# Weight sums by accumulating transfers in a seven-product feed-forward kernel

## The chip, the cores and the metric

One core of a Trainium2 chip runs the whole kernel in one launch. The metric is the device time of one execution in microseconds, the median of the runs shown.

## The reference

Two layers of a streaming encoder. Each layer adds half a SwiGLU, then a token mixer (a Mamba-2 scan of 8 heads and an HGRN2 scan of 4 heads, side by side, from one input projection and into one output projection), then half a second SwiGLU. All is float32, over 592 tokens (16 meta, 512 prompt, 64 sample) and 1024 features, with 2816 hidden features in each SwiGLU.

```python
def _swiglu(x, w_gate, w_up, w_down):
    return (jax.nn.silu(x @ w_gate) * (x @ w_up)) @ w_down
...
for l in range(DEPTH):
    h = h + 0.5 * _swiglu(_rmsnorm(h, ln_ffa_w[l]), ffa_w_gate[l], ffa_w_up[l], ffa_w_down[l])
    m, c, s, g = _mixer(_rmsnorm(h, ln_mix_w[l]), ...)
    h = h + m
    h = h + 0.5 * _swiglu(_rmsnorm(h, ln_ffb_w[l]), ffb_w_gate[l], ffb_w_up[l], ffb_w_down[l])
```

## The kernel before

**Products.** Activations lie with features on partitions and tokens along the free dimension. A float32 operand is split into a high part (`wh`, `qh`, type fp32r) and a low rest (`wl`, `ql`); each product is three matmuls: high by high, high by low, low by high (lines 649 to 651 and 675 to 677).

**Quads.** In a SwiGLU, blocks of weights and halves of activations are combined as in Strassen's and Winograd's method: a 2 by 2 block product takes seven products in place of eight. Such a step is a `Quad` (line 434). The order of its seven products and their operands is the list `QUAD`; `product_quad` (line 661) issues them into PSUM tiles `pq` (gate and up) or `pd` (down). Of the seven weight operands three are raw blocks (`g1`, `g2`, `u2`), and four are sums: `s1 = u1 + u2`, `s2 = s1 + g1`, `s4 = s2 + g2`, `s3 = g1 + u1`. A gate/up step covers one block of 128 hidden features; its weight blocks are 128 by 512 (256 KB). A down step covers two blocks of 128 output features, with weight blocks of 128 by 384 or 128 by 256 by the number of hidden chunks. The first two hidden blocks of a feed-forward block are plain jobs (`pg`, `pu`, line 642). A feed-forward block alternates stretches: gate/up steps until a group of hidden blocks is ready, then four down steps over the group.

**The weights' way.** `fetch` (line 506) runs through all jobs and, for a quad, `fetch_quad` (line 563) loads `g1`, `u1`, `u2`, `g2` with four SP transfers into `raw` tiles (`wr`, six buffers). `combine` (line 579) forms the four sums on VectorE into `zq` tiles (`ws`, four buffers). `convert` (line 588) makes of each operand the high part on ACT (line 598) into one of six `hi` tiles and the low part on VectorE (line 602) into one of six `lo` tiles; these come free when the product is issued. So a step has four sums and seven low parts on VectorE, and besides the evacuations: in a gate/up step lines 897 to 919, in a down step seven additions to `h` (line 1013). Gates make a product wait until the earlier content of its PSUM tile has been read.

**The order of work.** Every task is a Python generator that yields (engine, estimated ns, events to wait for, buffers needed). `Plan.run` (line 170) simulates the engines with these estimates at build time and emits each piece in the order in which it could start; that fixes the order of every engine's queue, SP's and POOL's included. On the chip the queues run in that order, and an instruction that waits holds those behind it. A tile of a tag takes one of the tag's buffers and waits for the release of what lay there.

**Mixer.** The convolution of one of eight channel tiles (`conv`, line 1142) writes a projected tile `u` and an accumulator `cacc`, both in the large pool `T` (52 buffers of 128 by 592), and ends with a Silu. `near` (line 1396) copies a query tile into `qd`, of which there is one buffer; it and `v_t` and `k_t` (one buffer each) also hold some of the hidden tiles of a feed-forward block. `states` (line 1452) loads a sample state `hss` from memory, then forms the final states in `hfin`. `load_scalars` (line 280) loads and prepares the small parameters.

Of the kernel before, what the change touches and what calls it, by code (L numbers as in the profile page):

```python
# [16 lines left out]
P = 128  # L17
# [20 lines left out]
BLK = ((0, 128), (128, 128), (256, 128), (384, 128), (512, 80))  # L38
NT = 52
UK = 4  # L40
# [157 lines left out]
def body(ctx: ExitStack, tc: tile.TileContext, a: dict, o: dict):  # L198
# [19 lines left out]
    bet = Buf(sb, "etot", 2, [P, 6], F32)  # L218
    bhs = Buf(sb, "hss", 2, [P, P], F32)
    bb = Buf(sb, "b_t", 2, [P, 256], F32)  # L220
# [59 lines left out]
    def load_scalars():  # L280
# [22 lines left out]

        t = yield V, 1500, (t,), (bT,)
        tmp = bT.tile("lbt", [P, 10, 4])
# [3 lines left out]
        V.tensor_tensor(sc[:, 1], r0, sc[:, 0], op=ALU.subtract)  # L309
        V.tensor_tensor(sc[:, 2], r1, sc[:, 0], op=ALU.subtract)  # L310
        S.activation(sc[:, 1:3], sc[:, 1:3], AF.Exp)
        V.tensor_tensor(sc[:, 3], sc[:, 1], sc[:, 2], op=ALU.add)
        V.reciprocal(sc[:, 3], sc[:, 3])
# [8 lines left out]
        V.tensor_scalar(lg[:, 1], lb, 1e-30, 2.0 ** -60, op0=ALU.max, op1=ALU.min)  # L322
        V.tensor_scalar(lg[:, 1], lg[:, 1], 2.0 ** 60, None, op0=ALU.mult)
        S.activation(lg, lg, AF.Ln)
        V.tensor_tensor(lna, lg[:, 0], lg[:, 1], op=ALU.add)
        V.tensor_scalar(nlna, lna, -1.0, None, op0=ALU.mult)
        V.tensor_scalar(lnc, lb, -1.0, 1.0, op0=ALU.mult, op1=ALU.add)
        S.activation(lnc, lnc, AF.Ln)
        bT.put(t + 1000)
        lb_ev.set(t + 1000)  # L330

# [66 lines left out]
    def near(order):  # L398
        return 1e-3 * order
# [106 lines left out]
    def fetch():  # L506
# [9 lines left out]
        for i, job in enumerate(jobs):  # L516
            if isinstance(job, Quad):
                yield from fetch_quad(i, job, chain)
                continue
            src = job.src.rearrange("(k p) c -> p k c", p=P)  # L520
            for k0, k1, u in job.units:
                if job.whole:
                    if i == 0:
                        yield from whole(i, job, src, k0, k1, u, chain)
                    else:
                        plan.add(near(job.order), whole(i, job, src, k0, k1, u, chain))
                    if i == 0:
                        for b, g in ((0, 1), (1, 1), (2, 1)) if k0 == 0 else ():
                            yield from fetch_x(b, g)
                    continue  # L530
                t = yield "DMA", 190 * (k1 - k0), (), (braw,)
                raw = braw.tile(f"wr{i}", [P, k1 - k0, src.shape[2]])
                SP.dma_start(raw, src[:, k0:k1])
                t += 2000.0
                if job.few:
                    plan.add(near(job.order), convert_few(i, job, u, raw, t, chain))
                else:
                    plan.add(near(job.order), convert(u, raw, chain, braw.put, t))
            if i == 1:
                for b, g in ((3, 0), (4, 0), (3, 1), (4, 1)):  # L540
                    yield from fetch_x(b, g)
                t = yield "DMA", 380, ()
                SP.dma_start(cf[:, P:], a["c_f"][:, P:3 * P])
                cf_ev.set(t + 2000)
                load_params()
# [11 lines left out]
    def scaled(norm, k0, k1, u, t):  # L557
# [3 lines left out]
        u.ready.set(t)  # L561

    def fetch_quad(i, job, chain):
        nk = job.mix.nk
        got = {}
        for name, src in (("g1", job.wg[0]), ("u1", job.wu[0]), ("u2", job.wu[1]), ("g2", job.wg[1])):
            t = yield "DMA", 190 * nk, (), (braw,)
            raw = braw.tile(f"wr{i}", [P, nk, P])
            SP.dma_start(raw, src)
            got[name] = [raw, Ev(), Ev({"g1": 3}.get(name, 2), braw.put)]  # L570
            got[name][1].set(t + 2000.0)
        for name, n in (("s1", 2), ("s2", 2), ("s4", 1), ("s3", 1)):
            got[name] = [None, Ev(), Ev(n, bzq.put)]
        plan.add(near(job.order), combine(i, nk, got))
        for k, ((name, _, _), u) in enumerate(zip(QUAD, job.units)):
            raw, ev, use = got[name]
            plan.add(near(job.order + k), convert(u, got[name], chain, use.set, ev))

    def combine(i, nk, got):
        for name, p, q in (("s1", "u1", "u2"), ("s2", "s1", "g1"), ("s4", "s2", "g2"), ("s3", "g1", "u1")):  # L580
            t = yield V, ns_dve(nk * P), (got[p][1], got[q][1]), (bzq,)
            dst = got[name][0] = bzq.tile(f"ws{i}", [P, nk, P])
            V.tensor_tensor(dst, got[p][0], got[q][0], op=ALU.add)  # L583
            got[name][1].set(t)
            got[p][2].set(t)
            got[q][2].set(t)

    def convert(u, raw, chain, done, *waits):
# [510 lines left out]
    def mixer(l, norm, nxt, hv_out):  # L1099
# [42 lines left out]
        def conv(c):  # L1142
# [3 lines left out]
            def sink(hf, sl, pt, t):  # L1146

                r = norm.rstd
                if hf == 0:
                    t = yield V, ns_dve(HT), (t, norm.done, col_ev["cw"]), (bT,)  # L1150
                    u = ut["u"] = bT.tile("u", [P, 601])
                    V.tensor_tensor(u[:, 3:3 + HT], pt, r[:, 0:HT], op=ALU.mult)
                    bmm.put(t)
                    ut["made"].set(t)
                    G.memset(u[:, 0:3], 0.0)
                    G.tensor_copy(u[:, 515:518], col["st"][:, 24 * l + c:24 * l + 24:8])
                    return
# [10 lines left out]
                cb = col["cb"][:, 8 * l + c:8 * l + c + 1]  # L1168
                t = yield (V, S), (501, ns_act(598) + 90), (t,), (bT,)
                acc = bT.tile("cacc", [P, 598])  # L1170
                if plan.pick == 0:
# [3 lines left out]
                for k in range(1, 4):  # L1175
                    t = yield V, ns_dve(650), (t,)
                    V.scalar_tensor_tensor(acc, u[:, k:k + 598], cw[k], acc, op0=ALU.mult, op1=ALU.add)
                bT.put(t)
                t = yield S, 880, (t,), (bT,)
# [3 lines left out]
                S.activation(dst[:, 576:592], acc[:, 582:598], AF.Silu)  # L1183
                bT.put(t)
                v = (x4 if c < 4 else bc4)[c % 4]
# [210 lines left out]
        def near(e, c):  # L1396


            t = yield (S, G), (ns_act(512), ns_pool(512)), (qev[c],), (bqd,)
            qd = bqd.tile(f"qd{c}")  # L1400
# [51 lines left out]
        def states(e, c):  # L1452

            t = yield "DMA", 200, (e.cum_ev,), (bhs,)
            e.ssam = bhs.tile("hss")
            SP.dma_start(e.ssam, a["state_hgrn"][l, 0, c])
            d = t + 2000
            t = yield PE, ns_mm(P, 6), (e.kt_ev, e.vt_ev), (baux, baux, bT, bT)
            e.st = bT.tile("hst", [P, 4, P])
            fin = bT.tile("hfin", [P, 2, P])  # L1460
            pn, p4 = baux.tile("pn"), baux.tile("pn4")
# [19 lines left out]
            SP.dma_start(o["hgrn_p"][l, 0, c], fin[:, 1])  # L1481
            bT.put(t + 2500)

        def outputs(e, c):
# [12 lines left out]
            bT.put(t, 2)  # L1497
            bhs.put(t)

# [498 lines left out]
```

## Time and profile before

| | |
|---|---|
| runs | 2338.93 us median of 3 (2338.72 to 2342.32) |
| profiled execution | 2340.86 us, span 2339.1 us |
| mean granted TensorE clock | 0.992 |
| TensorE matmul busy | 2268.3 us, 97% |
| TensorE weight load busy | 2183.7 us, 93% |
| VectorE (DVE) busy | 2027.6 us, 87% |
| ScalarE (ACT) busy | 1211.7 us, 52% |
| GpSimd (POOL) busy | 123.0 us, 5% |
| transfers | 188.28 MB, 28.1% of 16 engines' span on SP's queue |

The span goes from the first to the last instruction; the execution's own time is 1.8 us longer. Busy times are those of recorded instructions; matmuls overlap one another, and so do consecutive instructions of VectorE, so that durations add up to more than the time between starts. The rows on which the prediction rests stand below, after the change.

### The profile page before, as it was taken

How to read it: one execution, taken by the hardware profiler on the slowest of the kernel's cores; microseconds unless marked ns; L12 is line 12 of the kernel's file. 1: busy time of each engine (PE TensorE's matmuls, PEld its weight loads, DVE VectorE, ACT ScalarE, POOL GpSimd, SP SyncE). 2: the span in 40 equal slices, each digit the busy share in tenths (PEclk: the TensorE clock that was granted, in tenths of full speed). 3: DMA queues.
4: the chain of work that ended last, by engine and by line, in shares of the span. 5: the costliest groups of instructions: out<-in, count | busy, mean ns of one | idle time of the engine just before them, and what ended most of it. 6: DMA issues, size and time to landing. Idle time of an engine off the chain costs nothing.

```text
span 2339.1 us, 43538 instructions
## 1 busy us (share of the span) xinstructions
PE 2268.3 (97%) x16199; PEld 2183.7 (93%) x16199; DVE 2027.6 (87%) x4224; ACT 1211.7 (52%) x2486; POOL 123.0 (5%) x167
## 2 busy tenths in 40 slices
PE   8989999999899999999999999999998999999998
PEld 6989999999899899999979999999997998999998
DVE  6989989768976899998989999896789678999995
ACT  4545645546443355564545556464563534555653
POOL 0000000021300000000000000000212000000002
PEclk9999999999999999999999999999999999999999
DMA  4233332332112123323222323323311231233332
GB/s 119 82 96 88 87 95 77 96 80 60 31 43 82 55 82 100 91 82 100 74 71 85 101 86 90 92 81 92 82 44 33 57 89 55 82 109 91 87 98 75
DMA packets 370243, 188.28 MB, mean 80 GB/s; under 512 B 16544, under 2 KB 367568, under 8 KB 370032
## 3 DMA queue, kind: packets, MB, share of 16 engines
q1 hardware_dynamic: 370032, 185.50, 28.1%
q8 instruction: 128, 2.10, 0.4%
q14 instruction: 83, 0.68, 0.1%
HBM read 180.94 MB, written 4.51 MB: 79 GB/s over the span
## 4 chain that ended last, share of the span: by engine, by line
PE 61%; DVE 28%; DMA 6%; issue 4%; ACT 1%; SPq 0%; POOL 0%; DVEq 0%; ACTq 0%
PE pq L675 8%; PE pq L677 8%; PE pq L676 8%; DVE wl L602 7%; DVE ws L583 5%; PE pd L675 4%; PE pd L676 3%; PE pd L677 3%; DVE h L1013 3%; DMA wr<-in_ffa_w_up 2%; DMA wr<-in_ffb_w_up 2%; PE pa L1380 2%; PE px L649 1%; PE px L651 1%; PE px L650 1%
## 5 line engine op out<-in xcount | busy, mean ns | idle before, releaser
L598 ACT ACTIVATE wh<-ws 128x512 fp32r<-128x512 f32 (+2 forms) x560 | 321.8, 575 | 272.8 <-PE pd L676 119.0
L598 ACT ACTIVATE wh<-wr 128x512 fp32r<-128x512 f32 (+2 forms) x572 | 333.2, 587 | 218.0 <-PE pd L676 87.8
L602 DVE TENSOR_TENSOR wl<-wr,wh 128x512 fp32r<-128x512 f32 (+2 forms) x572 | 358.9, 640 | 6.4 <-ACT wh L598 4.4
L602 DVE TENSOR_TENSOR wl<-ws,wh 128x512 fp32r<-128x512 f32 (+2 forms) x560 | 339.2, 616 | 18.6 <-ACT wh L598 17.4
L675 PE MATMUL pd<-qh_g,wh 128*128 128x296 f32 (+1 forms) x1008 | 306.6, 304 | 11.6 <-DVE h L1013 7.8
L676 PE MATMUL pd<-ql_g,wh 128*128 128x296 f32 (+1 forms) x1008 | 301.8, 299 | 4.1 <-DVE ql_g L500 4.1
L677 PE MATMUL pd<-qh_g,wl 128*128 128x296 f32 (+1 forms) x1008 | 301.0, 299 | 0.0
L675 PE MATMUL pq<-qh_a,wh 128*128 128x296 f32 x960 | 287.6, 300 | 1.3 <-ACT u L889 1.3
L677 PE MATMUL pq<-qh_a,wl 128*128 128x296 f32 x960 | 286.4, 298 | 0.9 <-DVE wl L602 0.9
L676 PE MATMUL pq<-ql_a,wh 128*128 128x296 f32 x960 | 287.1, 299 | 0.2 <-DVE ql_a L500 0.2
L677 PE MATMUL pq<-qh_b,wl 128*128 128x296 f32 (+1 forms) x960 | 285.0, 297 | 0.9 <-DVE wl L602 0.9
L675 PE MATMUL pq<-qh_b,wh 128*128 128x296 f32 (+1 forms) x960 | 285.6, 297 | 0.0
L676 PE MATMUL pq<-ql_b,wh 128*128 128x296 f32 (+1 forms) x960 | 285.5, 297 | 0.0
L583 DVE TENSOR_TENSOR ws<-wr,wr 128x512 f32<-128x512 f32 (+2 forms) x280 | 172.8, 617 | 44.8 <-DMA wr<-in_ffa_w_up 21.3
L675 PEld LDWEIGHTS pd<-qh_g,wh 128*128 128x128 f32 x1008 | 190.7, 189 | 21.1 <-issue 15.1
L1013 DVE SCALAR_TENSOR_TENSOR h<-pd,h 128x296 f32<-128x296 f32 (+1 forms) x420 | 192.3, 459 | 11.1 <-PE pd L677 9.9
L676 PEld LDWEIGHTS pd<-ql_g,wh 128*128 128x128 f32 x1008 | 191.2, 190 | 4.7 <-DVE ql_g L500 4.7
L677 PEld LDWEIGHTS pd<-qh_g,wl 128*128 128x128 f32 x1008 | 191.0, 189 | 0.0
L676 PEld LDWEIGHTS pq<-ql_a,wh 128*128 128x128 f32 x960 | 180.9, 188 | 1.4 <-DVE ql_a L500 1.2
L677 PEld LDWEIGHTS pq<-qh_a,wl 128*128 128x128 f32 x960 | 180.7, 188 | 1.6 <-DVE wl L602 1.6
L675 PEld LDWEIGHTS pq<-qh_a,wh 128*128 128x128 f32 x960 | 180.4, 188 | 1.8 <-ACT u L889 1.5
L677 PEld LDWEIGHTS pq<-qh_b,wl 128*128 128x128 f32 x960 | 180.5, 188 | 1.7 <-DVE wl L602 1.7
(466 smaller groups left out, 5603.5 us busy)
## 6 DMA issues: line engine op xcount, KB each, us to landing
wr<-in_w_in SPq DMA_DIRECT2D x112, 256.0 KB, 3.1
wr<-in_ffa_w_gate SPq DMA_DIRECT2D x88, 256.0 KB, 3.0
wr<-in_ffa_w_up SPq DMA_DIRECT2D x88, 256.0 KB, 3.2
wr<-in_ffb_w_gate SPq DMA_DIRECT2D x88, 256.0 KB, 3.0
wr<-in_ffb_w_up SPq DMA_DIRECT2D x88, 256.0 KB, 3.2
wr<-in_ffa_w_down SPq DMA_DIRECT2D x96, 192.0 KB, 2.7
wr<-in_ffb_w_down SPq DMA_DIRECT2D x96, 192.0 KB, 2.7
wr<-in_w_out SPq DMA_DIRECT2D x32, 256.0 KB, 2.9
```

The costliest lines, as they stand in the source:

```text
L583: V.tensor_tensor(dst, got[p][0], got[q][0], op=ALU.add)
L598: S.activation(hi, raw, AF.Copy)
L602: V.tensor_tensor(u.lo[:, :u.n], raw, hi.bitcast(F32), op=ALU.subtract)
L649: PE.matmul(out[:, :n], u.hi[:, i], xh, start=(j == 0), stop=False)
L650: PE.matmul(out[:, :n], u.hi[:, i], xl, start=False, stop=False)
L651: PE.matmul(out[:, :n], u.lo[:, i], xh, start=False, stop=(j == nk - 1))
L675: PE.matmul(out, u.hi[:, j], xh, start=(new and j == 0), stop=False, skip_group_check=True)
L676: PE.matmul(out, u.hi[:, j], xl, start=False, stop=False, skip_group_check=True)
L677: PE.matmul(out, u.lo[:, j], xh, start=False, stop=(j == nk - 1), skip_group_check=True)
L1013: V.scalar_tensor_tensor(dst, sums[b], sign, dst, op0=ALU.mult, op1=ALU.add)
L1380: PE.matmul(pt[:n, c0 // 2:(c0 + n) // 2], ks[:, c0:c0 + n], qs[:, c0 // 2:(c0 + n) // 2], start=True, stop=True)
```

## The change

Five edits. (1) `s1` and `s3` are no longer formed on VectorE: for each, a task `load_sum` loads one addend with SP into a `zq` tile and then has POOL issue a transfer that adds the other addend onto it. `u1` is loaded twice, no longer as a raw tile; `s2` and `s4` stay on VectorE and go to `raw` tiles (`wt`). The raw loads of a step are issued after the VectorE sums of the step before have been emitted, and a `load_sum` after the one before it has emitted its load. (2) The buffer for descriptors of transfers issued by POOL grows from 256 to 2048. (3) In the convolution `u` goes to the one `qd` buffer and `cacc` to the one `v_t` buffer; `near` therefore waits for all Silus. (4) The `hss` buffers go; the sample state is loaded into a third part of `hfin`. `T` has one buffer more. (5) The preparation of the decay bounds in `load_scalars` is split into single-engine steps.

```diff
-NT = 52
+NT = 53
...
-    bhs = Buf(sb, "hss", 2, [P, P], F32)
...
-        t = yield V, 1500, (t,), (bT,)
+        t = yield V, 300, (t,), (bT,)
...
+        t = yield S, 100, (t,)
         S.activation(sc[:, 1:3], sc[:, 1:3], AF.Exp)
+        t = yield V, 1000, (t,)
...
+        t = yield S, 100, (t,)
         S.activation(lg, lg, AF.Ln)
+        t = yield V, 300, (t,)
...
+        t = yield S, 100, (t,)
         S.activation(lnc, lnc, AF.Ln)
...
-                t = yield "DMA", 190 * (k1 - k0), (), (braw,)
+                t = yield "DMA", 190 * (k1 - k0), (formed[0],), (braw,)
...
+    formed = [Ev(0)]
+
     def fetch_quad(i, job, chain):
+
         nk = job.mix.nk
+        src = {"g1": job.wg[0], "u1": job.wu[0], "u2": job.wu[1], "g2": job.wg[1]}
         got = {}
-        for name, src in (("g1", job.wg[0]), ("u1", job.wu[0]), ("u2", job.wu[1]), ("g2", job.wg[1])):
-            t = yield "DMA", 190 * nk, (), (braw,)
-            raw = braw.tile(f"wr{i}", [P, nk, P])
-            SP.dma_start(raw, src)
-            got[name] = [raw, Ev(), Ev({"g1": 3}.get(name, 2), braw.put)]
-            got[name][1].set(t + 2000.0)
-        for name, n in (("s1", 2), ("s2", 2), ("s4", 1), ("s3", 1)):
-            got[name] = [None, Ev(), Ev(n, bzq.put)]
-        plan.add(near(job.order), combine(i, nk, got))
+        for name, n in (("s1", 2), ("g1", 2), ("s3", 1), ("u2", 1), ("g2", 2), ("s2", 2), ("s4", 1)):
+            got[name] = [None, Ev(), Ev(n, (bzq if name in ("s1", "s3") else braw).put)]
+        before, formed[0] = formed[0], Ev()
+        for name, other in (("s1", "u2"), ("s3", "g1")):
+            prev, sums[0] = sums[0], Ev()
+            plan.add(near(job.order), load_sum(i, nk, src["u1"], src[other], got[name], prev, sums[0]))
+        plan.add(near(job.order), combine(i, nk, got, formed[0]))
...
-    def combine(i, nk, got):
-        for name, p, q in (("s1", "u1", "u2"), ("s2", "s1", "g1"), ("s4", "s2", "g2"), ("s3", "g1", "u1")):
-            t = yield V, ns_dve(nk * P), (got[p][1], got[q][1]), (bzq,)
-            dst = got[name][0] = bzq.tile(f"ws{i}", [P, nk, P])
+        for name in ("g1", "g2", "u2"):
+            t = yield "DMA", 190 * nk, (before,), (braw,)
+            raw = got[name][0] = braw.tile(f"wr{i}", [P, nk, P])
+            SP.dma_start(raw, src[name])
+            got[name][1].set(t + 2000.0)
+
+    sums = [Ev(0)]
+
+    def load_sum(i, nk, first, second, to, before, begun):
+        t = yield "DMA", 190 * nk, (before,), (bzq,)
+        dst = to[0] = bzq.tile(f"ws{i}", [P, nk, P])
+        SP.dma_start(dst, first)
+        begun.set(0.0)
+        t = yield G, 1000, (t + 2500.0,)
+        G.dma_start(dst, second, accum_op=ALU.add)
+        to[1].set(t + 4500.0)
+
+    def combine(i, nk, got, formed):
+        for name, p, q in (("s2", "s1", "g1"), ("s4", "s2", "g2")):
+            t = yield V, ns_dve(nk * P), (got[p][1], got[q][1]), (braw,)
+            dst = got[name][0] = braw.tile(f"wt{i}", [P, nk, P])
             V.tensor_tensor(dst, got[p][0], got[q][0], op=ALU.add)
             got[name][1].set(t)
             got[p][2].set(t)
             got[q][2].set(t)
+        formed.set(0.0)
...
-                    t = yield V, ns_dve(HT), (t, norm.done, col_ev["cw"]), (bT,)
-                    u = ut["u"] = bT.tile("u", [P, 601])
+                    t = yield V, ns_dve(HT), (t, norm.done, col_ev["cw"]), (bqd,)
+                    u = ut["u"] = bqd.tile("u", [P, 601])
...
-                t = yield (V, S), (501, ns_act(598) + 90), (t,), (bT,)
-                acc = bT.tile("cacc", [P, 598])
+                t = yield (V, S), (501, ns_act(598) + 90), (t,), (bvt,)
+                acc = bvt.tile("cacc", [P, 598])
...
-            t = yield (S, G), (ns_act(512), ns_pool(512)), (qev[c],), (bqd,)
+            t = yield (S, G), (ns_act(512), ns_pool(512)), (qev[c], silu_in), (bqd,)
...
-            t = yield "DMA", 200, (e.cum_ev,), (bhs,)
-            e.ssam = bhs.tile("hss")
+            t = yield "DMA", 200, (e.cum_ev,), (bT,)
+            fin = bT.tile("hfin", [P, 3, P])
+            e.ssam, e.fin_use = fin[:, 2], Ev(2, bT.put)
...
-    nc = _bacc.Bacc("TRN2", target_bir_lowering=False, num_devices=1, dynamic_dma_scratch_size=256)
+    nc = _bacc.Bacc("TRN2", target_bir_lowering=False, num_devices=1, dynamic_dma_scratch_size=2048)
```

## Rows read from the trace of the kernel before

**Rows 1.** Two stretches: window, length, busy (xcount) of PE, PEld, DVE, ACT, POOL; clock, DMA share, GB/s.

```profile
1388.90:1457.60 68.70, 68.70 (x507) 68.70 (x506) 66.93 (x127) 42.57 (x84) 0.00 (x0) 1.00 0.32 92
2265.10:2298.60 33.50, 33.50 (x254) 33.43 (x253) 27.17 (x48) 19.65 (x38) 0.00 (x0) 1.00 0.33 95
```

**Rows 2.** The same view, the four feed-forward blocks.

```profile
54.00:436.00 382.00, 365.62 (x2607) 358.58 (x2606) 352.38 (x739) 213.82 (x430) 1.35 (x4) 0.99 0.31 87
814.50:1184.00 369.50, 363.02 (x2606) 356.11 (x2605) 347.77 (x714) 202.73 (x406) 0.00 (x0) 1.00 0.31 91
1221.50:1590.40 368.90, 362.18 (x2606) 355.48 (x2605) 351.01 (x722) 210.84 (x425) 0.00 (x0) 1.00 0.31 88
1967.60:2298.60 331.00, 328.33 (x2438) 323.72 (x2437) 311.79 (x622) 185.19 (x364) 0.00 (x0) 1.00 0.32 93
```

**Rows 3.** The chain of waits in the first feed-forward block, shares by line.

```profile
by line: DVE wl L602 13.3%; DMA wr<-in_ffa_w_up 9.6%; DVE ws L583 9.5%; PE pq L675 8.1%; PE pq L677 8.0%; PE pq L676 7.9%; issue 6.6%; DVE h L1013 5.5%; PE pd L675 5.3%; PE pd L676 4.5%; PE pd L677 4.4%; DMA wr<-in_ffa_w_down 3.0%; DVE ql_g
```

**Rows 4.** Busy time by window again: the start, and single stretches.

```profile
0.00:54.00 54.00, 43.05 (x176) 32.86 (x176) 35.88 (x73) 25.36 (x53) 3.02 (x7) 0.94 0.48 129
...
54.00:114.40 60.40, 58.49 (x422) 57.40 (x421) 59.62 (x114) 36.02 (x73) 0.00 (x0) 1.00 0.28 79
114.40:158.40 44.00, 36.68 (x254) 35.98 (x253) 34.56 (x79) 16.63 (x30) 1.35 (x4) 0.92 0.36 100
...
205.70:231.60 25.90, 25.06 (x170) 23.24 (x170) 24.55 (x65) 12.80 (x28) 0.00 (x0) 1.00 0.35 103
...
396.60:436.00 39.40, 36.75 (x254) 35.87 (x254) 38.33 (x88) 27.55 (x59) 0.00 (x0) 0.96 0.31 81
...
1552.70:1590.40 37.70, 35.55 (x254) 34.44 (x253) 37.63 (x87) 27.19 (x59) 0.00 (x0) 1.00 0.32 85
1967.60:2026.10 58.50, 57.88 (x422) 56.08 (x421) 58.29 (x113) 35.58 (x72) 0.00 (x0) 1.00 0.28 82
```

**Rows 5.** VectorE's groups of line 583: shapes, xcount, busy us, mean ns, idle before.

```profile
L583 DVE TENSOR_TENSOR ws<-wr,wr 128x512 f32<-128x512 f32 x160 | 109.7, 686 | 36.9 <-DMA wr<-in_ffa_w_up 21.3 <-DMA wr<-in_ffb_w_up 15.0 <-DVE wl L602 0.5
...
L583 DVE TENSOR_TENSOR ws<-wr,wr 128x384 f32<-128x384 f32 x96 | 53.1, 553 | 6.5 <-DMA wr<-in_ffa_w_down 3.0 <-DMA wr<-in_ffb_w_down 2.9
...
L583 DVE TENSOR_TENSOR ws<-wr,wr 128x256 f32<-128x256 f32 x24 | 10.1, 419 | 1.4 <-DMA wr<-in_ffa_w_down 1.2
```

**Rows 6.** VectorE's timeline at two places: start us, duration us, line, operation.

```profile
964.12 0.41 DVE L583 TENSOR_TENSOR ws<-ws,wr 128x256 f32<-128x256 f32 x1
964.45 0.42 DVE L583 TENSOR_TENSOR ws<-wr,wr 128x256 f32<-128x256 f32 x1
...
1013.18 0.69 DVE L602 TENSOR_TENSOR wl<-ws,wh 128x512 fp32r<-128x512 f32 x1
1013.78 0.47 DVE L904 SCALAR_TENSOR_TENSOR u<-pq,u 128x296 f32<-128x296 f32 x1
```

**Rows 7.** Waits of SP's queue, TensorE and VectorE: us in total, times, longest.

```profile
SPq L569 <- DVE wl L602: 728.3, 231, 16.8
...
PE pd L675 <- DVE h L1013: 12.6, 15, 7.1
...
DVE ws L583 <- DMA wr<-in_ffa_w_up: 21.3, 16, 7.2
```

**Rows 8.** Transfers: SP's queue (packets, MB, share of 16 engines); one issue (KB, us to landing).

```profile
q1 hardware_dynamic: 370032, 185.50, 28.1%
...
wr<-in_ffa_w_up SPq DMA_DIRECT2D x88, 256.0 KB, 3.2
```

**Rows 9.** VectorE's timeline in the convolutions.

```profile
476.83 0.46 DVE L1152 TENSOR_TENSOR u<-px,rs_m 128x296 f32<-128x296 f32 x1
477.21 0.83 DVE L1177 SCALAR_TENSOR_TENSOR cacc<-u,par_c,cacc 128x598 f32<-128x598 f32 x1
```

**Rows 10.** ACT's timeline in the scalar task; idle before and releaser in brackets.

```profile
161.67 1.28 ACT L324 ACT_TABLE_LOAD   x1
...
164.19 0.21 ACT L328 ACTIVATE lnc<-lnc 128x8 f32<-128x8 f32 x1 [0.51 <-DVE lnc L327]
```

More of the change, by code (lines that the diff above doesn't have):

```diff
@@ L327, in load_scalars @@
         V.tensor_scalar(lnc, lb, -1.0, 1.0, op0=ALU.mult, op1=ALU.add)
+        t = yield S, 100, (t,)
         S.activation(lnc, lnc, AF.Ln)
-        bT.put(t + 1000)
-        lb_ev.set(t + 1000)
+        bT.put(t)
+        lb_ev.set(t)
     h = res.tile([P, KD, T], F32, name="h")
@@ L1177, in sink @@
                     V.scalar_tensor_tensor(acc, u[:, k:k + 598], cw[k], acc, op0=ALU.mult, op1=ALU.add)
-                bT.put(t)
+                bqd.put(t)
                 t = yield S, 880, (t,), (bT,)
@@ L1183, in sink @@
                 S.activation(dst[:, 576:592], acc[:, 582:598], AF.Silu)
-                bT.put(t)
+                bvt.put(t)
                 v = (x4 if c < 4 else bc4)[c % 4]
@@ L1452, in states @@
         def states(e, c):
-            t = yield "DMA", 200, (e.cum_ev,), (bhs,)
-            e.ssam = bhs.tile("hss")
+            t = yield "DMA", 200, (e.cum_ev,), (bT,)
+            fin = bT.tile("hfin", [P, 3, P])
+            e.ssam, e.fin_use = fin[:, 2], Ev(2, bT.put)
             SP.dma_start(e.ssam, a["state_hgrn"][l, 0, c])
             d = t + 2000
-            t = yield PE, ns_mm(P, 6), (e.kt_ev, e.vt_ev), (baux, baux, bT, bT)
+            t = yield PE, ns_mm(P, 6), (e.kt_ev, e.vt_ev), (baux, baux, bT)
             e.st = bT.tile("hst", [P, 4, P])
-            fin = bT.tile("hfin", [P, 2, P])
             pn, p4 = baux.tile("pn"), baux.tile("pn4")
@@ L1481, in states @@
             SP.dma_start(o["hgrn_p"][l, 0, c], fin[:, 1])
-            bT.put(t + 2500)
+            e.fin_use.set(t + 2500)
         def outputs(e, c):
@@ L1497, in outputs @@
             bT.put(t, 2)
-            bhs.put(t)
+            e.fin_use.set(t)
             t = yield S, 5 * ns_act(P), (t,), (bT, bT)
```

## The prediction

> **What bounds the kernel now.** I began with the page's busy shares: TensorE 97%, VectorE 87%. A busy TensorE is not a TensorE at its peak, because its matmuls overlap, so I counted matmuls. In two stretches where it never stood still, one 296-column matmul took 68.70 us / 507 = 135.5 ns, and one of 288 columns, in the last block, 33.50 / 254 = 131.9 ns [rows 1]. These are my full rate (135.6 and 131.9 below). The rest of a stretch is lost time, whatever the busy column says.
>
> Next the four feed-forward blocks, from the first seven-product step to the last down product that one window still covers [rows 2]. Count times full rate, taken from the length: 382.0 - 2607 x 0.1356 = 28.5 us; 369.5 - 353.4 = 16.1; 368.9 - 353.4 = 15.5; 331.0 - 2438 x 0.1319 = 9.4. Together **69.5 us**: nothing done to the weights' path inside these blocks can give more.
>
> Then who is late there. In the first block the chain of waits runs through `wl`, through the weight sums `ws` and through the loads of `in_ffa_w_up` at least as much as through the products [rows 3]. The shorter stretches say where [rows 4]. In the first gate/up stretch of a block VectorE is busy 59.62 of 60.40 us, in the two-chunk down stretch 24.55 of 25.90, in a block's last down stretch 38.33 of 39.40. One stretch is of another kind: 44.00 us for 254 matmuls, with the granted clock at a mean of 0.92 and VectorE at 34.56.
>
> **The sums on VectorE.** The sums `s1` and `s3`, raw plus raw, go: 160 + 96 + 24 = 280 instructions, 172.9 us of recorded durations [rows 5]. `s2` and `s4` stay. Durations overlap, so what the queue gains is the spacing of starts [rows 6]: 0.60 us at 512 columns (1013.18 to 1013.78 us), 0.33 at 256 (964.12 to 964.45), and so some 0.47 at 384, half way. Where VectorE sets the pace:
> - First gate/up stretch, four times: 60.40 - 422 x 0.1356 = 3.2 us lost in the first block, 2.8 in the last [rows 4], some 11.5 in all. Five steps shed 10 x 0.60 = 6.0 us of VectorE, so it stops leading. The split of the activations remains; I take 8.5.
> - Two-chunk down, three times: 25.90 - 170 x 0.1356 = 2.8 each, 8.5. VectorE sheds 8 x 0.33 = 2.6 each; I take 7.
> - Last down stretch of a block, three times: 5.0 in the first, 3.3 in the third [rows 4], some 11.3. VectorE sheds 8 x 0.47 = 3.8 each, but the next norm's squares and splits stay; I take 6.5.
> - The 44.00 us stretch lost 9.6. VectorE's longest wait for `in_ffa_w_up`, 7.2 us, lies here [rows 7]; the granted clock then fell to the lower of its two levels, 1.2 in place of 2.4 GHz, for some 7 us (0.08 x 44 = 3.5 us lost), as the tail of that wait. The scalar task's many small transfers ahead of these weights stay, so between 0 and 9.6; weights will be further ahead, and I take 4.
> - Everything else in [rows 2], 69.5 - 11.5 - 8.5 - 11.3 - 9.6 = 28.6 us, is waits of one or two us: for an evacuation behind other VectorE work, for `up` weights behind a buffer. I take two fifths, 11, since the sums are one of several causes.
>
> Gain: 8.5 + 7 + 6.5 + 4 + 11 = **37 us**, between 0 and 69.5.
>
> **The weights' path.** A step now loads five plain blocks in place of four (`u1` twice) and accumulates two. A 256 KB block is 512 packets of 512 B, 32 on each of 16 engines; a packet occupied its engine 0.281 x 2339.1 us x 16 / 370032 = 28.4 ns [rows 8]. Five plain loads are 160 x 28.4 ns = 4.5 us of a step that lasts 84 x 0.1356 = 11.4 us. No accumulating packet is in the trace. From below it costs a plain packet: 64 x 28.4 = 1.8 us, 6.3 in all. From above I allow 5 packets, 9.1 us, 13.6 in all, which no longer fits. I take two packets, 3.6 us, nearest to the only row there is, since the tile has to be read as well as the weights: 8.1 of 11.4, hidden behind the products. Without that cover each step would cost the excess.
>
> The Trainium skill has the rule for that second read: Collectives: The Full Stack, section "The bandwidth ceiling: the fold count and why AG ≠ RS ≠ AR", holds that a reduction in flight pays nothing for the addition itself but fetches two operands for each result, and runs at half a copy's rate; by it the step would also be 8.1 us, by a plain packet's price 6.3. No run here shows it.
>
> Latency: a sum needs a load (3.2 us [rows 8]) and then an issue on POOL and an accumulation, both unseen: together at least another load's 3.2 us; from above I allow three times that, so 6.4 to 12.8 us in all; I take 8. The four `zq` tiles hold two steps' sums, so each tile comes round every 22.8 us; covered. The raw loads wait less: `g1`, which `s3` also held, is free after `s2`. Now SP waits 728.3 us for `wl` before raw loads [rows 7], most of it harmless. If the accumulation ran late, `wh` of `s1` is late next, then `s2`, and ACT's conversions behind it.
>
> POOL: two issues per step on a queue idle in these blocks (1.35 us in the whole first one, 0 in the others [rows 2]). Each waits for its own first load, so the norm's `pow`, queued behind it, can lose up to a load, 3.2 us, at each block's head, and the activations' sums behind that; between 0 and 13 us for four, and at the start SP and the transfers are busiest (0.48 of the transfer engines' time before 54 us [rows 4]). I put **7 us** on the four heads: 3 for the first, 2 for the third, 1 each for the others.
>
> **The moved tiles.** With one `u` and one `cacc` buffer, the next tile's first product half (476.83 us) must wait for the last tap of the one before (477.21 to 478.04) [rows 9]: 1.2 us later, hidden by the other three of the four PSUM tiles that take a half each. Without that cover, 8 x 2 x 1.2 = 19 us at most; I take 0. `hss` inside `hfin` holds a `T` tile longer, with one `T` tile added: 0, cover the added tile; its load stays on SP, and if no tile is free the `w_in` loads behind it wait. `near` waits for the Silus; its product waits for later things anyway: 0.
>
> **The scalars.** Now ACT is held from 161.67 to 164.4 us: a table load of 1.28, and two waits for VectorE, of which the second, 0.51, is shown [rows 10]. In steps the waits go; a Silu between may bring two more loads. Between -1.0 (both waits) and +2.6 (two loads), I take 0.
>
> **Sum.** -37 + 7 = -30 us. The profiled execution took 2340.86, 1.9 over the median shown, so the median comes to 2338.9 - 30 = **2309 us**.
>
> **Rivals.**
> - *The transfers become the bound* (slower). Place: the ring of transfer engines in every step. Decides from (11.4 - 4.5) us / 64 = 107 ns an accumulating packet, 3.8 plain ones. At 128 ns a gate/up step takes 12.7 us: +1.3 x 80 steps, +1.0 x 48 of three chunks, +0.65 x 12 of two (the counts are half of [rows 5]), 160 us on the floor of 2338.9 - 69.5 = 2269: 2430. For it: no row has the price. Against: 0.31 of the engines' time is used now. 0.14.
> - *POOL's descriptor work is the bound* (slower): decides from 5.7 us an issue; at 7, 2.6 x 80 + 2.0 x 48 + 1.3 x 12 = 320 over the floor, 2590. 0.03. Against: in these blocks the sums and `u` are two-input instructions [rows 5, 6], and POOL has nothing else. By the Trainium skill, SBUF — State Buffer, the box "The DVE blocks DMA trap" under "SBUF: two separate sides", POOL cannot write descriptors while VectorE runs a copy that takes both ports; the groups named are not such copies, and no run here has such an issue.
> - *TensorE was the bound anyway*, 97% busy; the gains are small evacuation waits and the heads eat them: 2339. For it: its own waits named for `h` are 12.6 us in the whole run [rows 7]. 0.09.
> - *All of the lost time comes back* and the heads cost nothing: 2269. Against: the gates between products stay. 0.11.
>
> **How the numbers follow.** The forecast has 0.63, with 2285 to 2330 of its own (gain 10 to 55). Faster by over 0.2% (4.7 us, about what a measurement of this kernel can tell from no change) is 0.63 + 0.11 = 0.74, within 0.09, slower 0.14 + 0.03 = 0.17. The range, 2276 to 2345, leaves out the two slower cases and a little of the last.
>
> **What would show it.** Right: raw-plus-raw sums gone, VectorE near 1855 us busy, first gate/up stretches under 58.5 us, two-chunk down under 24, and the four blocks some 35 us shorter. Wrong: transfer share above 0.8 in these blocks, `wh` or `s2` waiting for accumulations, POOL busy for several us an issue, `pow` late at block heads, or `u` waiting in the mixer.

## The result and the profile after

The changed kernel took 2375.53 us (median of four runs, 2373.06 to 2383.15) where the kernel before, run beside it, took 2340.62. The ratio is 1.0152, with a 95% interval of 1.0129 to 1.0174. I had forecast 2309 and a range up to 2345: 35 us slower came where I expected 30 us faster. The profiled run took 2373.9 us, its span 2372.1, 33.0 over the span of before.

First the four feed-forward blocks of the changed kernel by window, in the columns of [rows 2]:

```profile
49.60:439.00 389.40, 367.39 (x2607) 359.97 (x2606) 326.20 (x677) 220.60 (x439) 88.56 (x72) 0.99 0.71 145
822.20:1200.30 378.10, 363.71 (x2606) 357.35 (x2605) 319.58 (x647) 202.85 (x406) 90.88 (x71) 1.00 0.74 152
1236.70:1612.70 376.00, 364.28 (x2606) 358.10 (x2605) 322.83 (x656) 211.50 (x427) 87.09 (x68) 0.99 0.73 148
1993.00:2330.70 337.70, 328.28 (x2438) 323.65 (x2437) 285.54 (x560) 185.52 (x364) 77.41 (x60) 1.00 0.75 155
```

Against [rows 2] each block is longer, by 7.4, 8.6, 7.1 and 6.7 us: 29.8 of the 33.0. VectorE, third of the busy columns, sheds 26 to 28 us a block, as meant, and TensorE does not gain from it. The transfer engines' share rises from 0.31 to between 0.71 and 0.75. Outside the blocks the two mixers take 4.7 and 3.1 us more and the start 4.4 less.

Which stretches? The first and the six-step gate/up stretch of the first block:

```profile
49.60:111.30 61.70, 59.50 (x423) 57.51 (x422) 58.48 (x119) 40.72 (x81) 10.29 (x8) 1.00 0.66 140
...
230.60:305.70 75.10, 71.14 (x505) 70.65 (x505) 59.12 (x111) 43.17 (x85) 18.10 (x14) 0.97 0.76 151
```

The first was 60.40 [rows 4]. The second, in the kernel before:

```profile
231.60:301.40 69.80, 69.27 (x506) 68.61 (x506) 65.72 (x126) 41.64 (x84) 0.00 (x0) 1.00 0.32 91
```

It was 69.80 us and is 75.10 now, with VectorE busy for 59.12 us of it: VectorE isn't short of time, it is late. The other blocks' first stretches came down from 59.9, 60.1 and 58.5 us to 58.6, 59.1 and 57.4. The three two-chunk down stretches, 25.8 to 25.9 us before, grew to 28.6, 26.8 and 28.1.

Who is late stands in VectorE's groups of line 605 (the two sums that stay), with busy time, mean ns and idle time ahead:

```profile
L605 DVE TENSOR_TENSOR wt<-ws,wr 128x512 f32<-128x512 f32 x80 | 55.1, 689 | 113.8 <-DMA ws<-in_ffb_w_up 45.6 <-DMA ws<-in_ffa_w_up 44.5 <-issue 12.7
L605 DVE TENSOR_TENSOR wt<-wt,wr 128x512 f32<-128x512 f32 x80 | 54.8, 685 | 0.9
```

`s2` needs the transferred `s1`, and VectorE stood idle for 113.8 us ahead of 80 such instructions. `s4`, of `s2` and a raw tile, waits for nothing. Before, VectorE's worst wait of the kind was 21.3 us in all [rows 7].

One case in full. VectorE, ScalarE and TensorE in the timeline, with idle time and releaser in brackets:

```profile
249.68 0.69 DVE L605 TENSOR_TENSOR wt<-ws,wr 128x512 f32<-128x512 f32 x1 [3.40 <-DMA ws<-in_ffa_w_up]
250.29 0.46 DVE L942 SCALAR_TENSOR_TENSOR gg<-pq,gg 128x296 f32<-128x296 f32 x1
...
250.78 0.70 ACT L502 ACTIVATE qh_g<-gg 128x592 fp32r<-128x592 f32 x1 [2.69 <-DVE gg L942]
251.38 0.40 ACT L912 ACTIVATE u<-pq 128x296 f32<-128x296 f32 x1
...
249.32 0.30 PE L700 MATMUL pq<-qh_a,wl 128*128 128x296 f32 x1
251.84 0.40 PE L698 MATMUL pq<-qh_a,wh 128*128 128x296 f32 x1 [2.22 <-ACT u L912]
252.08 0.34 PE L699 MATMUL pq<-ql_a,wh 128*128 128x296 f32 x1
252.21 0.45 PE L700 MATMUL pq<-qh_a,wl 128*128 128x296 f32 x1
252.46 0.45 PE L698 MATMUL pq<-qh_a,wh 128*128 128x296 f32 x1
```

VectorE stands 3.40 us in front of `s2` until `s1` lands. Behind it is `gg`, which ScalarE's split waits for, 2.69 us; behind that is the evacuation `u`, and TensorE waits 2.22 us for it. Soon after the pause matmuls last 0.45 us in place of 0.30. The window over them has the granted clock last but two, 0.50:

```profile
252.20:255.60 3.40, 3.40 (x16) 3.40 (x15) 3.40 (x7) 2.01 (x5) 0.61 (x1) 0.50 0.88 152
```

That is the lower of TensorE's two levels (1.2 in place of 2.4 GHz), for 3.4 us after a pause of 2.2, and part of the 0.97 in the stretch's row. No weight was missing on TensorE; a sum that is late held two in-order queues.

The transfers themselves, by queue and by issue:

```profile
q1 hardware_dynamic: 434736, 217.49, 33.5%
q0 software_dynamic: 129408, 63.98, 22.1%
...
ws<-in_ffa_w_up SPq DMA_DIRECT2D x80, 256.0 KB, 3.9
...
ws<-in_ffa_w_up POOLq DMA_DIRECT2D x40, 256.0 KB, 5.4
ws<-in_ffa_w_gate POOLq DMA_DIRECT2D x40, 256.0 KB, 5.7
```

A packet of POOL's queue occupied its engine for 0.221 x 2372.1 us x 16 / 129408 = 64.8 ns, 2.3 times the plain packet of [rows 8].

### The profile page after: what moved, and what is told of

Same layout as the page of the kernel before. It is cut to its first block, busy times and chain, and to the rows that moved or that the text cites. A ratio compares the mean times of both kernels' runs of the same rounds, so it can differ in the third digit from the quotient of the medians.

```text
span 2372.1 us, 44224 instructions
## 1 busy us (share of the span) xinstructions
PE 2277.6 (96%) x16199; PEld 2191.5 (92%) x16199; DVE 1903.7 (80%) x3939; ACT 1217.8 (51%) x2493; POOL 496.8 (21%) x449
## 3 DMA queue, kind: packets, MB, share of 16 engines
q0 software_dynamic: 129408, 63.98, 22.1%
## 5 line engine op out<-in xcount | busy, mean ns | idle before, releaser
L621 ACT ACTIVATE wh<-ws 128x512 fp32r<-128x512 f32 (+2 forms) x280 | 160.6, 574 | 144.8 <-PE pd L699 66.5
L621 ACT ACTIVATE wh<-wt 128x512 fp32r<-128x512 f32 (+2 forms) x280 | 160.7, 574 | 132.8 <-PE pd L699 61.1
L698 PEld LDWEIGHTS pq<-qh_b,wh 128*128 128x128 f32 x960 | 181.4, 189 | 10.0 <-ACT u L912 7.1
L625 DVE TENSOR_TENSOR wl<-ws,wh 128x512 fp32r<-128x512 f32 (+2 forms) x280 | 172.2, 615 | 19.4 <-ACT wh L621 19.2
L605 DVE TENSOR_TENSOR wt<-ws,wr 128x512 f32<-128x512 f32 (+2 forms) x140 | 86.6, 618 | 120.9 <-DMA ws<-in_ffb_w_up 45.6
```

Source lines behind the costliest of these rows:

```text
L621: S.activation(hi, raw, AF.Copy)
L625: V.tensor_tensor(u.lo[:, :u.n], raw, hi.bitcast(F32), op=ALU.subtract)
L698: PE.matmul(out, u.hi[:, j], xh, start=(new and j == 0), stop=False, skip_group_check=True)
```

## The experiments

Each ratio is to the kernel before, run beside it on the same chip; brackets hold its 95% interval. Theory **L** is the one of the case above: sums land late and hold the in-order queues. **C**: the transfers crowd each other; **M**: the moved parts and the order; **Q** and **Z** came after the first four runs and are told there.

**Without the accumulations.**

```
         t = yield G, 1000, (t + 2500.0,)
-        G.dma_start(dst, second, accum_op=ALU.add)
```

> The changed kernel with the accumulating transfers alone left out: s1 and s3 are then plain copies of u1, which changes the values and not the order of any engine's instructions. Theory L (late sums: VectorE and ScalarE stand in their own order behind sums whose accumulation lands some 5 us after its issue, and evacuations behind them hold TensorE): the waits of wt for ws go, the four feed-forward blocks shorten by about 30 to 60 us in all, 2310 to 2345. Theory C (the transfers themselves, 0.7 of the engines' time, delay every weight): also 2310 to 2345, so this run doesn't part L from C. Theory M (the moved conv tiles, the scalars and the order that the planner now chooses are the loss): 2365 to 2376, nothing changes in the blocks.

2305.47 us, ratio 0.9879 [0.9864, 0.9894]. The blocks and the stretch that took 75.10 us:

```profile
50.70:415.70 365.00, 359.73 (x2607) 355.25 (x2606) 327.36 (x677) 221.96 (x439) 2.45 (x4) 1.00 0.40 113
803.70:1163.00 359.30, 358.11 (x2607) 355.40 (x2606) 320.32 (x646) 204.67 (x406) 0.00 (x0) 1.00 0.40 116
1197.20:1557.90 360.70, 358.91 (x2606) 354.97 (x2605) 324.05 (x656) 212.86 (x427) 0.00 (x0) 1.00 0.39 112
1938.10:2262.70 324.60, 324.55 (x2439) 323.15 (x2438) 287.03 (x560) 186.75 (x364) 0.00 (x0) 1.00 0.41 118
...
218.50:287.10 68.60, 68.60 (x507) 68.60 (x506) 59.88 (x112) 42.87 (x84) 0.00 (x0) 1.00 0.40 116
```

The six-step stretch is at the full rate (507 x 0.1356 = 68.7). Against [rows 2] the blocks gain 17.0, 10.2, 8.2 and 6.4 us, 42 together, near the 37 that I had forecast for them. The accumulations, then, take back 42 + 30 = 72 us in the blocks, more than the 30 to 60 that I expected under L. Between L and C the run doesn't decide; for the blocks M doesn't hold.

**The parts alone.** The moved tiles and scalars without the sums, and the sums without these:

> The kernel before with every part of the change but the sums (u and cacc in their new buffers, the state tile in hfin, near's wait, the scalars in steps, 53 T tiles, the larger scratch). The mixers grew by 4.7 and 3.1 us in the changed kernel; if they grew because of the moved tiles, this run shows it: theories L and C 2342 to 2352 (+0 to +8 on the kernel before, with 0 to 4 back from the scalars). Theory M: 2360 to 2376.

> The kernel before with the transferred sums alone (51 T tiles in place of 52, since u and cacc stay in T tiles, the larger scratch, all else as before). Theories L and C: 2365 to 2380, the whole loss without the mixers' 8 us. Theory M: 2310 to 2335, the gain I forecast.

1.0058 [1.0039, 1.0077] and 1.0092 [1.0072, 1.0112]. The two add up to the change's 1.5%, and both are losses. My expectation for the sums alone was too dark (2355.46 us where the kernel before took 2332.56 on that chip) and the moves cost more than the 8 us that L allowed (2345.02, 12.5 over it).

**The planner's latencies.** The planner places an instruction by when it believes its input is there:

```
-        t = yield G, 1000, (t + 2500.0,)
+        t = yield G, 1000, (t + 4200.0,)
-        to[1].set(t + 4500.0)
+        to[1].set(t + 6000.0)
```

> The changed kernel with only the planner's two latencies set nearer to what the trace measures: 4200 ns in place of 2500 from the issue of a sum's load to its landing, 6000 in place of 4500 for the accumulation. The same transfers, another order of instructions: wt is queued about 3 us later. Theory L: part of the waits of wt (104 us in the named rows) goes from VectorE's queue, 2340 to 2368. Theory C: the transfers are the same, so 2370 to 2380. Theory M: unclear, within 10 us of the changed kernel.

1.0049 [1.0033, 1.0065], as L has it: the same transfers, and two thirds of the loss come back. But the six-step stretches of the first three blocks rose, from 75.1, 73.9 and 73.3 to 75.3, 78.2 and 75.5 us, and the very first stretch from 61.7 to 68.0, while most others fell. POOL's timeline in a six-step stretch, and the `s2` between:

```profile
229.02 1.29 POOL L598 DMA_DIRECT2D ws<-in_ffa_w_up  x1 [4.55 <-issue]
234.78 1.30 POOL L598 DMA_DIRECT2D ws<-in_ffa_w_gate  x1 [4.47 <-DVE gg L920]
240.05 1.29 POOL L598 DMA_DIRECT2D ws<-in_ffa_w_up  x1 [3.96 <-issue]
245.33 1.30 POOL L598 DMA_DIRECT2D ws<-in_ffa_w_gate  x1 [3.99 <-DVE wl L625]
...
234.54 0.69 DVE L605 TENSOR_TENSOR wt<-ws,wr 128x512 f32<-128x512 f32 x1 [0.65 <-DMA ws<-in_ffa_w_up]
...
245.04 0.69 DVE L605 TENSOR_TENSOR wt<-ws,wr 128x512 f32<-128x512 f32 x1 [0.55 <-DMA ws<-in_ffa_w_up]
```

`s2` starts the moment `s1` has landed, at 234.54 and 245.04, and each time POOL issues `s3` 0.24 and 0.29 us later. `s3` doesn't need `s1`: its issue waited for the accumulation before it. The releasers named in the brackets change from row to row, some are "issue": a wait that no semaphore explains. The issues come 5.8, 5.3 and 5.3 us apart, two to a step of 11.4. I counted it over the changed kernel: between two gate/up accumulations in a row, 140 pairs, the second issue started a median 0.65 us after the last packet of the first had ended (quartiles 0.62 and 0.67), and never under 4 us after the first issue. So they go **one at a time**. Theory Q: POOL's descriptor scratch, 2048 bytes, doesn't hold two blocks' descriptors. Theory Z: the `zq` tiles or the loads ahead set that pace.

The changed kernel's down sums, in smaller blocks, speak for Q:

```profile
111.68 2.59 POOL L598 DMA_DIRECT2D ws<-in_ffa_w_down  x2 [16.06 <-DVE lb L318]
...
ws<-in_ffa_w_down POOLq DMA_DIRECT2D x48, 192.0 KB, 4.9
```

Here two issues follow each other within 2.59 us, and a block of 192 KB takes a median 4.9 us to land. Of the 120 down accumulations 70 were issued 0.3 us or more before another one landed; of the 160 of 256 KB every one came after the landing of the one ahead. So two can be in flight on POOL's queue; it is the larger blocks that go singly.

**256 bytes more.**

```
-dynamic_dma_scratch_size=2048
+dynamic_dma_scratch_size=2304
```

> The changed kernel with one number changed: the descriptor scratch of the transfers that POOL issues, 2304 bytes in place of 2048. In the trace of the changed kernel an accumulating issue of a 256 KB block starts a median 0.65 us after the last packet of the one before has ended (25th to 75th percentile 0.62 to 0.68), so they go one at a time, some 5.3 us each, 10.6 of the 11.4 us of a step. Theory Q (the scratch doesn't hold the descriptors of two 256 KB blocks, and POOL waits for room): the two issues of a step come under 4 us apart, sums land earlier, the six-step gate/up stretches (73 to 75 us) shorten to under 71, 2325 to 2355. Theory Z (the pace is set by the four zq tiles coming free and by the load ahead of each accumulation): the spacing stays above 5 us and the time within 2362 to 2376.

0.9988 [0.9971, 1.0004]: this one number takes back the loss. Of the 140 pairs 75 now come under 4 us apart. POOL in the same stretch, and that stretch by window:

```profile
232.46 1.28 POOL L598 DMA_DIRECT2D ws<-in_ffa_w_up  x1 [7.50 <-DMA ws<-in_ffa_w_up]
233.23 1.84 POOL L598 DMA_DIRECT2D ws<-in_ffa_w_gate  x1
242.70 1.29 POOL L598 DMA_DIRECT2D ws<-in_ffa_w_up  x1 [7.63 <-DVE wt L605]
243.50 1.83 POOL L598 DMA_DIRECT2D ws<-in_ffa_w_gate  x1
...
227.00:296.00 69.00, 69.00 (x506) 69.00 (x506) 59.56 (x111) 42.84 (x84) 15.55 (x12) 0.99 0.76 157
```

The two issues of a step follow each other at once and POOL then rests 7.5 us; the stretch is 69.00 in place of 75.10, and the other four are between 66.8 and 69.1. Z falls. The order of the instructions is that of the changed kernel, so M has no part in it.

**Both numbers.** Scratch of 2304 and the latencies:

> Both: the scratch of 2304 bytes and the planner's latencies of 4200 and 6000 ns. With real latencies alone the short stretches were already at the full rate and the six-step stretches were worse, 75 to 78 us. Theory Q: these fall below 71, and the whole comes to 2315 to 2330, the moved tiles' 13 us over the run without accumulations at most. Theory Z: 2340 to 2350, as with the real latencies alone.

2310.69 us, 0.9871 [0.9852, 0.9891]. The six-step stretch of the first block:

```profile
223.10:291.60 68.50, 68.50 (x506) 68.50 (x505) 60.60 (x114) 43.84 (x87) 18.21 (x14) 1.00 0.85 172
```

At the full rate, with the transfers' share at 0.85. The whole is below the range that I gave, and level with the run that had no accumulations (0.9879), though not part by part: the order of instructions differs. The four blocks take 1420.2 us against 1409.6 there, the mixers 757.2 against 768.2. Of the blocks' 10.6 us the first stretch has 7.2, the other two six-step stretches of 296 columns (70.4 and 70.8 us) about 4. The first stretch here and without accumulations:

```profile
49.80:117.70 67.90, 61.45 (x423) 59.48 (x422) 62.27 (x129) 43.81 (x84) 14.68 (x15) 0.97 0.64 137
```

```profile
50.70:111.40 60.70, 59.20 (x422) 57.48 (x421) 58.49 (x118) 40.66 (x81) 2.45 (x4) 1.00 0.39 110
```

It holds eleven VectorE instructions more, besides more traffic; which of them costs the 7.2 us isn't shown. So theory C is not what lost the 72 us, since all of the traffic is there; that it costs nothing anywhere isn't shown.

**Without the moved parts too.** Only the sums, scratch 2304, the latencies:

> The sums alone, without the moved tiles and the scalars (51 T tiles), with the scratch of 2304 bytes and the latencies of 4200 and 6000 ns. Theory Q with the moves as a separate loss of some 13 us: 2300 to 2318 where the kernel before stands at 2333, so faster than both. Theory Z: 2325 to 2340.

2299.71 us beside 2339.82, 0.9824 [0.9804, 0.9845]: **faster than both kernels**, and just below the range expected. Its very first stretch is still 73.0 us, 12.6 over the kernel before; there VectorE waits 6.9 us for `cm`, a piece of POOL's work in the scalar task, and TensorE 7.8 for an evacuation. More room still, 4096 bytes with 50 `T` tiles, gave nothing beyond it, 0.9836 [0.9818, 0.9855]:

> The sums alone with the real latencies, as the run that stood at 0.9824 [0.9804, 0.9845], but with 4096 bytes of scratch in place of 2304 and 50 T tiles in place of 51. If a third and fourth block's room helps the first gate/up stretch (73.0 us) and the longest ones (69 to 71): 0.978 to 0.982. If room for two blocks was all that was wanted: 0.981 to 0.986.

**A plain load on POOL's queue** in place of the accumulation, scratch 2048:

> The changed kernel, scratch of 2048 bytes, with POOL's second transfer into each sum's tile a plain load in place of an accumulation: the same bytes, queue and order, and s1 and s3 become u2 and g1 alone. If the adding in flight is the cost (64.8 ns a packet in the changed kernel, 29.7 a plain one): as without the accumulations, a ratio of 0.987 to 0.992. If room for descriptors is (theory Q): the next issue still waits for the last packet of the one before, only the stream between is shorter, some 4.3 us a block in place of 5.3: the ratio falls from 1.015 to between 1.000 and 1.010.

0.9869 [0.9848, 0.9889], the edge of the first alternative by its number, and still no answer, since a premise failed: they were not the same packets. POOL's queue of this run:

```profile
q0 software_dynamic: 20096, 63.98, 9.2%
```

The plain block went in packets eight times as large, so in an eighth as many, and 76 of the 140 pairs came under 4 us apart within 2048 bytes. It fits Q, and it doesn't price the addition. So I asked for the limit itself:

> The changed kernel with 2112 bytes of scratch in place of 2048. A 256 KB block is 512 accumulating packets, 32 on each of 16 engines. Theory Q with each packet needing two source entries and one block one entry more, at 16 bytes an entry (the entry's size is the Trainium skill's, DMA: Bandwidth & Descriptors, section Terms, an estimate): 65 entries, 1040 bytes a block, 2080 for two, more than 2048 and less than 2112. Then this run is as the one with 2304: ratio 0.996 to 1.001, over half of the gate/up issues under 4 us apart. If the limit lies elsewhere between 2112 and 2304: 1.013 to 1.017 and no issue under 4 us, as in the change.

1.0000 [0.9987, 1.0012], with 76 of 140 pairs under 4 us apart: 64 bytes do what 256 did. The change's scratch misses two blocks by 64 bytes at most. The Trainium skill, DMA: Bandwidth & Descriptors, section Terms, gives a descriptor 16 bytes, kept in rings in SBUF; the estimate of 2080 bytes for two blocks rests on that and on the guess of two source entries a packet. By the same estimate a 192 KB block takes 784 bytes, so that two of them, or one beside a 256 KB block (1824), fit into 2048, as the down sums did. The runs place the limit for two 256 KB blocks between 2048 and 2112; no run shows the entries.

**The mixers.** Which of the moved parts costs 0.4 to 0.6%? Each from the kernel before:

> The kernel before with the conv tiles alone moved (u to the single qd buffer, cacc to the single v_t buffer, and near's wait for the Silus that goes with it). The three parts together, without the sums, gave a ratio of 1.0058 to the kernel before. If the single buffers and near's wait are the cause: 1.004 to 1.007. If it is the state tile, the T tile added or the scalars: 0.998 to 1.002.

1.0041 [1.0020, 1.0062], so the conv tiles. The state tile, the scalars and `cacc` alone:

> The kernel before with the state tile alone moved into hfin (hss in a T tile, 52 T tiles). The conv tiles alone gave 1.0041 [1.0020, 1.0062], the three parts together 1.0058 [1.0039, 1.0077]. If the rest of it is the state tile: 1.001 to 1.003; if not: within 0.999 to 1.001.

> The kernel before with the scalars alone in single-engine steps. I forecast 0, between -1.0 and +2.6 us: a ratio of 0.9996 to 1.0011. If the steps set ScalarE back in the first block: up to 1.003.

> The kernel before with cacc alone moved to the single v_t buffer; u stays in T tiles and near does not wait. If the single buffer that the taps run in is the cause of the conv tiles' 0.4%: 1.003 to 1.006. If u's single buffer or near's wait is: 0.999 to 1.002.

0.9991 [0.9976, 1.0005], 0.9999 [0.9987, 1.0012], 1.0000 [0.9988, 1.0011]: nothing in any of them. Left were `u`'s single buffer and the wait that came with it:

```
-            t = yield (S, G), (ns_act(512), ns_pool(512)), (qev[c],), (bqd,)
+            t = yield (S, G), (ns_act(512), ns_pool(512)), (qev[c], silu_in), (bqd,)
```

> The kernel before with near's wait for the Silus alone; u, cacc and the state tile where they were. If near's later place in the planner's order is the cost of the moved conv tiles: 1.003 to 1.006. If u's single buffer is: 0.999 to 1.002.

> The kernel before with u in the single qd buffer and near's wait, cacc left in a T tile. Since cacc alone cost nothing (1.0000), the conv tiles' cost should be here in full whichever of the two causes it: 1.003 to 1.006. If it takes both single buffers together: 0.999 to 1.002.

> The conv tiles moved as in the change, but with two qd buffers, so that u has a second one (51 T tiles pay for it). If u's single buffer is the cost: 0.998 to 1.002. If near's wait is: 1.003 to 1.006, as with one buffer.

1.0053 [1.0035, 1.0071] for the wait alone, 1.0070 [1.0049, 1.0092] with `u`, 1.0045 [1.0028, 1.0061] with a second buffer. It is `near`'s wait; a second buffer for `u` doesn't take it away. Whether `u`'s single buffer adds to it isn't shown: 1.0070 is above what I expected, but the two intervals overlap, and no run has it without the wait. The two mixers, from the first `q` product to the next block, before and with the wait alone:

```profile
436.00:814.60 378.60, 369.69 (x2693) 349.76 (x2692) 290.13 (x629) 174.15 (x380) 52.10 (x66) 1.00 0.23 63
1590.40:1967.60 377.20, 368.17 (x2693) 348.68 (x2692) 288.42 (x628) 173.63 (x380) 52.14 (x71) 0.99 0.23 63
```

```profile
434.10:818.80 384.70, 373.69 (x2694) 352.99 (x2692) 287.11 (x626) 174.93 (x382) 63.81 (x67) 0.99 0.23 62
1591.70:1976.70 385.00, 372.77 (x2692) 352.75 (x2692) 286.71 (x626) 173.70 (x381) 60.80 (x72) 0.98 0.23 62
```

They took 755.8 us before and 769.7 with the wait alone; in the changed kernel, which has the wait among other things, 763.5; in the run of 0.9824, which has no such wait, 748.3.

One place where the wait bites: POOL's small `pow` of the output norm with the wait, VectorE beside it, and POOL's in the kernel before:

```profile
573.34 7.00 POOL L1510 TENSOR_TENSOR st_o<-st_o,mhalf 128x4 f32<-128x4 f32 x2 [9.96 <-DVE st_o L1507]
...
573.24 0.81 DVE L1342 TENSOR_TENSOR ks<-cum 128x288 f32<-128x288 f32 x2
573.98 0.44 DVE L1344 TENSOR_TENSOR ks<-cum,cmk 128x288 f32<-128x288 f32 x1
574.35 0.77 DVE L1349 TENSOR_TENSOR qs<-ks,q 128x256 f32<-128x256 f32 x2
```

```profile
594.45 2.42 POOL L1510 TENSOR_TENSOR st_o<-st_o,mhalf 128x4 f32<-128x4 f32 x2 [4.49 <-DVE st_o L1507]
```

Two small instructions take 7.00 us while VectorE runs a row of two-input instructions without a gap; before, another order put them elsewhere, and they took 2.42. In every kept trace with the wait four `pow` instructions take 5.2 to 6.5 us, in every one without it none takes over 1.6. The Trainium skill, SBUF — State Buffer, section Who interferes with whom, says that VectorE's second SBUF input comes over a read port that POOL shares, and that one then blocks the other; the row agrees. Who waits for it, in the run with the wait:

```profile
ACT yt L1513 <- POOL st_o L1510: 18.7, 8, 3.7
...
PE oT L1520 <- ACT yt L1513: 10.1, 4, 2.8
```

Before, TensorE had no such wait, and ScalarE's was:

```profile
ACT yt L1513 <- POOL st_o L1510: 4.0, 6, 1.2
```

These 10.1 of the mixers' 13.9 us are named. That they are lost in full is not shown; for the rest there are only lower granted clocks in some windows (0.99 and 0.98 in the mixers' rows, 1.00 and 0.99 before), which I didn't follow.

## Why the prediction was wrong

**Right.** The gain in sum: 42 us in the blocks without accumulations against my 37. Its parts were not, so that some of the closeness is luck: the first stretches gave 3.2 us (8.5 forecast), the two-chunk ones 4.0 (7), the last ones of a block 4.5 (6.5), the 44.00 us stretch 7.2 (4), and all the rest 23 (11). The full rate, and that the lost time lay in VectorE's queue. The packet: 64.8 ns against my 56.8, far from the 107 where transfers would bind, so that rival was wrong; by the rule of a second read, as I cited it from the Trainium skill, Collectives: The Full Stack, a packet costs twice a plain one, and the trace agrees with 2.3. POOL's work: 1.3 us an issue against the 5.7 of the second rival. The scalars, 0. Of my signs of being wrong `s2` waiting for accumulations came.

Of the signs of being right most failed. One first gate/up stretch fell under 58.5 us (57.4), the two-chunk ones grew, and VectorE fell to 1903.7 us and not to 1855: for that sign I had taken off whole durations, which overlap; my own spacings give about 1879. The 7 us on the heads did not come either: in all VectorE waits 8.1 us for the norms' `pow`, as before the change, and the start and the head of the third block were 4.4 and 1.1 us shorter.

**Wrong, first: the latency step.** I put a sum at 8 us (6.4 to 12.8), and one block's is in that range: 3.9 to 4.5 us of load and 5.2 to 5.7 from issue to landing. The error is the next sentence, that each `zq` tile comes round every 22.8 us and the latency is "covered". I counted tiles and engine time as the only resources, and priced the two sums of a step as if they ran side by side. They ran one at a time in a scratch whose size stands in the diff, 5.3 us each, 10.6 of 11.4; `s3` so comes after its own load and two accumulations. I gave that line no term in the sum. It is worth 1.0152 to 0.9988.

**Wrong, second: "late next".** I named what would be late if the accumulation were, but not what stands behind it in order. The planner's 2500 and 4500 ns were in the diff as well, and against 3.9 and 5.4 they put `s2` into VectorE's queue too early. With room for the descriptors, true latencies are worth another 1.2% (0.9988 to 0.9871).

**Wrong, third: `near` at 0.** "Its product waits for later things anyway" may be right of the product, which no run shows, and is beside the point: in an order made by a planner a wait moves everything placed after it. Alone it cost 0.5%, some 12 to 14 us, within the 19 I had kept for `u` and `cacc`; `cacc`'s buffer costs nothing that could be measured, and for `u`'s no cost of its own is shown.

The end on which I put 0.17, slower, came by none of its two mechanisms.

## What to carry to other kernels

A transfer is bound by more than bytes, packets and tiles: ask how many of them the issuing engine can hold in flight, and look in the trace for issues that start right after the last one ended, with a releaser that makes no sense. Where a planner orders in-order queues, a latency that it believes too short is paid by whatever is queued behind the wait, mostly something unrelated. And a wait added to one task isn't priced at that task: compare the orders.

## What the hardware showed that I had not expected

- Two accumulating blocks of 256 KB are in flight together with 2112 bytes of descriptor scratch, and never with 2048; of 192 KB blocks two are, with 2048.
- On POOL's queue the same bytes went in 512-byte packets when accumulating and in 4096-byte ones when plain (129408 against 20096 packets), at 22.1 against 9.2% of the transfer engines' time.
- With the transfer engines at a share of 0.85, TensorE held its full rate for 68.5 us (in two like stretches it lost about 2).
- A POOL instruction of 128 x 4 elements, 1.0 to 1.5 us in the kernel before, lasted 6.49 us beside VectorE's two-input row (7.00 with the 80 x 1 instruction behind it).
